# A hybrid state-space and attention block: two input buffers and an own output tile for the state-space units, units 14 steps apart, and the mixing's first loads two steps sooner

## The chip, the cores and the metric

The kernel runs on one core of a Trainium2 chip, whose engines work side by side: TensorE for matmuls (PE in the profile; its weight loads are PEld), VectorE (DVE), ScalarE (ACT), GpSimd (POOL), and SyncE (SP), which here issues most DMA transfers, one after the other. The metric is device time in microseconds, lower is better. The kernel before takes 2308.74 us, the median of three runs (2308.12 to 2310.45).

## What is computed

One layer on x of 2048 tokens by 1024, cut to what matters here:

```python
h = rmsnorm(x, norm_mix_g)
proj = h @ w_in                       # 512 columns u, then q, k, v of 512 each
# A: 32 groups of 16 channels, each with a complex diagonal state of 64
bu = einsum('bsgh,gph->bsgp', u, b_bar)
states = associative_scan(combine, (lam_bar, bu))
y = einsum('bsgp,ghp->bsgh', states, c_mat).real + d_skip * u
y = gelu(y)
y_ssm = y * sigmoid(y @ w_glu + b_glu)          # the GLU
# B: 8 heads; every chunk of 64 frames attends to itself and the 8 before it
y_att = chunked_attention(q, k, v, rel_bias)
x = x + concat(rmsnorm(y_ssm), rmsnorm(y_att)) @ w_out
h2 = rmsnorm(x, norm_ffn_g)
x = x + (silu(h2 @ w_gate) * (h2 @ w_up)) @ w_down
return rmsnorm(x, norm_final_g)
```

All is float32. A matmul is done as three matmuls on operands that are split into a rounded part and a rest (the names ending in h and l, or hi and lo).

## The kernel before

The projection of u comes first. Then `att_phase` runs the attention as 128 steps (token block, head pair, head, quarter of the block), with s as the number of the loop's turn. Each turn makes, in the order "sptf": the scores of step s (tile `sc`; bias and minimum on DVE, exp on ACT), every fourth turn the product of probabilities and V (`pj`) or its scaling, the transposes of step s − 2 (`pt`, one bank; ACT casts it to `pth`, DVE makes the rest `ptl`), and then "f": every `Unit` is advanced. A `Unit` is a generator with a number of yields n, a first turn s0 and an end s1: its yields are spread evenly over the turns from s0 to s1, and with `pre` its first piece comes that many turns ahead of s0. The units of the q, k and v projections (`pf`) are PE's filler between the attention steps. The order of PE is that of the code; the other engines' order is decided by the scheduler.

The state-space part is eight units of four groups each (`ssm_unit`). A unit loads its u into the tile `U`, and the weights `Bst`, `Tm` and `Vm`, all by SP (helper at L567, Tm and Vm at L576 to L581). After `YL` = 8 yields come the matmuls `pj<-U,Bst` (here "X"), copied by ACT into the tile `X` (L591). GpSimd scans it in seven local steps and fourteen more pieces (L605 to L617), DMAs put the shifted states into `XG` (L639), and after `YX` = 9 yields the matmuls `pj<-U,Tm` and `pj<-XG,Vm` ("Y") read U a second time. ACT copies them (L649) into a tile of the same tag as `X`, and SP stores it to y in DRAM in eight pieces (L652). The pool `sp` has one buffer for each tag, so U, and the tile that is X and then Y, are shared by all units. Unit b runs from turn 2 + 15b to turn 17 + 15b. X and Y use the two `pj` banks of the attention.

At turn `OPEN` = 119 the pool `aw` is given back and `mix_phase` begins; its first piece loads the gains and the GLU weights (`load_wg`, `sg` to `wgh` and `wgl`) and stops at a yield. At turn `GSTART` = 122 the pool `sp` is given back; from there the unit of the mixing runs, to turn 130. It loads the y of the first block in four pieces (`yr`, L1030), applies gelu (L1034, the second time for the block behind it), loads the attention's output `ya` (L1044, stored at L899) and the first `w_out` rows, yields `PY` = 8 times, and then gives PE one group of three GLU matmuls (`pf<-gh,wgh`) at a yield: 16 groups. The bias (L1061), one sigmoid over all groups and the product (L1065) end it. The row scaling of the attention's output is at L1082. Behind the attention the mixing goes on with the next block's GLU (`big`) and the norm's reciprocal root (L115 to L123).

Of the kernel before, what the change touches and what calls it, by code (L numbers as in the profile page):

```python
# [16 lines left out]
P = 128  # L17
# [3 lines left out]
NG, CH, NS = 32, 16, 64  # L21
NPR = NG // 2
L = 8
NC = SEQ // L
GB, GP = 4, 2
# [6 lines left out]
EPS = 1e-6  # L32
LAG = 2
WB = 3
OPEN, GSTART = 119, 122
R1 = 13
SGB = 2
ON_POOL = 2, 5, 7
# [6 lines left out]
SL = 1  # L45
LPH = 2
V0 = 0, 4
DB, XB = 3, 2
SW = 15
CUT = -8, -2, 2, 7, 13, 19, 24  # L50
CUTL = -8, -2, 2, 7, 13, 19, 23
ORDER = "sptf"
# [1 line left out]
YL = 8  # L54
YX = 9
# [504 lines left out]
def ssm_unit(k, p, psum, S, b, eng):  # L560

    nc = k.nc
    F = GB * CH
    U = k.t(p, "U", [P, GB, NC])

    def load(out, in_):
        ins = nc.sync.dma_start(out, in_)  # L567
        if b == 0:
            k.tc.keep_in_program_order(ins)

    for j in range(L):
        load(U[j * CH : (j + 1) * CH], S["u"][b * F : (b + 1) * F, j, :].rearrange("(g c) t -> c g t", c=CH))
    gs = slice(GB * b, GB * b + GB)
    bst = k.t(p, "Bst", [P, GB, P])
    load(bst[:].rearrange("p g m -> p (g m)"), S["bst"][b // 2][:, (b % 2) * GB * P : (b % 2 + 1) * GB * P])
    tm = k.t(p, "Tm", [P, GB, P])  # L576
    for i in range(L):
        load(tm[i * CH : (i + 1) * CH], S["kt"].rearrange("c g a m -> c g (a m)")[:, gs, P - CH * i : 2 * P - CH * i])
    vm = k.t(p, "Vm", [P, GB, P])
    load(vm[:], S["v"].rearrange("q g c n m -> (c n) (q g) m")[:, gs, CH:])  # L580
    for _ in range(YL):  # L581
        yield

    X = k.t(p, "X", [P, 2, GP, NC])
    for q in range(GP):
        ps = k.t(psum, "pj", [P, 2, NC], bufs=2)
        for g2 in range(2):
            k.ta.matmul(ps[:, g2, :], bst[:, 2 * q + g2, :], U[:, 2 * q + g2, :], start=True, stop=True)
        for g2 in range(2):
            for c in range(2):  # L590
                nc.scalar.copy(X[g2 * NS : (g2 + 1) * NS, c, q, :], ps[c * NS : (c + 1) * NS, g2, :])  # L591
        yield

    a8 = S["a8"]
    qs = slice(GP * b, GP * b + GP)
    Xk = X[:].rearrange("p r q (k s) -> p r q k s", s=8)
    Xe = Xk[:, :, :, :, 7].rearrange("p r q (a b) -> p r q a b", b=8)

    def step(dst, src, e, n):

        ar = a8[:, 0, qs, (0, 7, 15)[e]].unsqueeze(1).to_broadcast([P, 2, GP]).unsqueeze(3).to_broadcast([P, 2, GP, n])
        aw = S["sw"][:, e, :, qs].unsqueeze(3).to_broadcast([P, 2, GP, n])
        t = k.t(p, "st1", [P, 2, GP, NC // 8])
        t2 = k.t(p, "st2", [P, 2, GP, NC // 8])
        eng.tensor_tensor(t[:, :, :, :n], src, ar, op=ALU.mult)  # L605
        eng.tensor_tensor(t2[:, :, :, :n], src[:, ::-1], aw, op=ALU.mult)
        eng.tensor_tensor(dst, dst, t[:, :, :, :n], op=ALU.add)
        eng.tensor_tensor(dst, dst, t2[:, :, :, :n], op=ALU.add)

    def carry(dst, end, i0, n):  # L610

        for c in range(2):
            for e in range(2):
                t = k.t(p, "fx", [P, GP, NC // 8, 7])[:, :, :n]
                pw = a8[:, c if e == 0 else 1 - c, qs, i0 : i0 + 7].unsqueeze(2).to_broadcast([P, GP, n, 7])
                eng.tensor_tensor(t, end[:, e].unsqueeze(3).to_broadcast([P, GP, n, 7]), pw, op=ALU.mult)
                eng.tensor_tensor(dst[:, c], dst[:, c], t, op=ALU.subtract if e == 1 and c == 0 else ALU.add)  # L617
            yield

    for s in range(1, 8):  # L620
        step(Xk[:, :, :, :, s], Xk[:, :, :, :, s - 1], 0, NC // 8)
        yield
    for b_ in range(1, 8):
        step(Xe[:, :, :, :, b_], Xe[:, :, :, :, b_ - 1], 1, 4)
        yield
    for a in range(1, 4):
        step(Xe[:, :, :, a : a + 1, 7], Xe[:, :, :, a - 1 : a, 7], 2, 1)
        yield
    yield from carry(Xe[:, :, :, 1:, :7], Xe[:, :, :, :3, 7], 8, 3)
    yield from carry(Xk[:, :, :, 1:, :7], Xk[:, :, :, : NC // 8 - 1, 7], 0, NC // 8 - 1)  # L630

    if b == 0:
        k.XG = k.t(p, "XG", [P, GB, NC])
        nc.gpsimd.memset(k.XG[:, :, 0:1], 0.0)
    XG = k.XG
    XGv = XG[:].rearrange("p (q g) c -> p q g c", g=2)
    for g2 in range(2):
        for c in range(2):
            eng.dma_start(XGv[c * NS : (c + 1) * NS, :, g2, 1:], X[g2 * NS : (g2 + 1) * NS, c, :, : NC - 1])  # L639
    for _ in range(YX):  # L640
        yield
    Y = k.t(p, "X", [P, GB, NC])
    for q in range(GP):
        ps = k.t(psum, "pj", [P, 2, NC], bufs=2)
        for g2 in range(2):
            g = 2 * q + g2
            k.ta.matmul(ps[:, g2, :], tm[:, g, :], U[:, g, :], start=True, stop=False)
            k.ta.matmul(ps[:, g2, :], vm[:, g, :], XG[:, g, :], start=False, stop=True)
        nc.scalar.copy(Y[:, 2 * q : 2 * q + 2, :], ps[:])  # L649
        if q == GP - 1:  # L650
            for j in range(L):
                nc.sync.dma_start(S["y"][b * F : (b + 1) * F, j, :].rearrange("(g c) t -> c g t", c=CH), Y[j * CH : (j + 1) * CH])  # L652
        yield


SSM_N = YL + GP + 7 + 7 + 3 + 4  + YX + GP


class Unit:
# [21 lines left out]
def att_phase(k, ident, S):  # L681
    tc, nc, io = k.tc, k.nc, k.io
    with ExitStack() as cx:
# [245 lines left out]
        sp = tc.alloc_tile_pool(name="ssm", reuse_waits="tile", bufs=1)  # L929
        psum = cx.enter_context(tc.tile_pool(name="aps", bufs=1, space=bass.MemoryType.PSUM, reuse_waits="tile"))  # L930
        psum2 = cx.enter_context(tc.tile_pool(name="aps2", bufs=1, space=bass.MemoryType.PSUM, reuse_waits="tile"))
        units = []
# [9 lines left out]
                      Unit(qk_unit(sb, 2), QK_N, g0 + C[3], g0 + C[4], 2, light=LIGHT), Unit(v_unit(sb, 1), V_N, g0 + C[4], g0 + C[5], 2, light=LIGHT),  # L942
                      Unit(qk_unit(sb, 3), QK_N, g0 + C[5], g0 + C[6], 2, light=LIGHT)]
        for b in range(NG // GB):
            units.append(Unit(ssm_unit(k, sp, psum, S, b, k.ssm_eng), SSM_N, 2 + int(SW * b), 2 + int(SW * (b + 1)), light=SL))
        N = len(steps)
        for s in range(N + LAG + 2):
            if s == OPEN:
                aw.release()
                mix = mix_phase(k, S, lambda: k.t(pfs, "pf", [P, 512]))  # L950
                units += [Unit(islice(mix, MIX_N), MIX_N, GSTART, N + LAG, GSTART - OPEN)]
            if s == GSTART:
                sp.release()
            for o in ORDER:
                if o == "s" and s < N:
                    scores(steps[s])
                elif o == "t" and LAG <= s < N + LAG:
                    transp(steps[s - LAG])
                elif o == "p" and LAG + 1 <= s < N + LAG + 1 and steps[s - LAG - 1][3] == 3:
                    pv_head(steps[s - LAG - 1])  # L960
                elif o == "p" and s >= LAG + 2 and steps[s - LAG - 2][2:] == (1, 3):
                    pv_scale(steps[s - LAG - 2])
                elif o == "f":
                    for u in units:
                        u.advance(s)
        return mix


PY, PZ = 8, 1
MIX_N = 17 + PY + PZ  # L970


def mix_phase(k, S, bank):

    tc, nc, io = k.tc, k.nc, k.io
    te = k.te
    with ExitStack() as cx:
# [3 lines left out]
        gs, ga, bg = (k.t(mz, n, [P, 4]) for n in ("gs", "ga", "bg"))  # L981
# [40 lines left out]
        def load(sb, one=False):  # L1022
            b = B()
            b.o = {}
            yt = k.t(my, "ys", [P, 4, SB], bufs=2)
            b.ys, b.g = [yt[:, f] for f in range(4)], []
            if sb % 2 == 0:
                yrs[0] = k.t(my, "yr", [P, 4, L, 128])
                for f in range(4):
                    nc.sync.dma_start(yrs[0][:, f], S["y"][f * P : (f + 1) * P, :, sb * 64 : sb * 64 + 128])  # L1030
            yv = b.yr = yrs[0][:, :, :, (sb % 2) * 64 : (sb % 2 + 1) * 64]
            fs = [slice(0, 4)] if one else [slice(f, f + 1) for f in range(4)]
            for s in fs:
                nc.scalar.activation(yt[:, s].rearrange("p f (c j) -> p f c j", j=L), yv[:, s].rearrange("p f j c -> p f c j"), AF.Gelu_apprx_tanh)  # L1034
            for f in range(4):
                gh, gl = k.t(my, f"gh{f}", [P, SB], F32R), k.t(my, f"gl{f}", [P, SB], F32R)
                split(k, gh[:], gl[:], b.ys[f], nc.vector)
                b.g.append((gh, gl))
            return b
# [102 lines left out]
                    yield t[:, i * SB : (i + 1) * SB]  # L1142

        load_wg()
        yield
        mw = rx.enter_context(tc.tile_pool(name="mw", reuse_waits="tile", bufs=2, side="right"))
        wr = rx.enter_context(tc.tile_pool(name="wr", reuse_waits="tile", bufs=2, side="right"))
        b = load(0, True)
# [25 lines left out]
        psum, mx = k.psum, k.mx  # L1174
# [6 lines left out]
        for sb in range(NSB):  # L1181
# [39 lines left out]
            b = nxt  # L1221
# [483 lines left out]
```

## Time and profile before

| | us |
|---|---|
| median of three runs | 2308.74 |
| the profiled execution | 2304.9 |
| its span, first to last instruction | 2303.1 |
| scores of turn 119 begin | 684.84 |
| Y of unit 7 begins | 691.00 |
| first GLU matmul | 713.61 |
| first GLU matmul of the next block (`big`) | 743.35 |

Times inside the execution are from the start of the span. A timeline row gives start, duration, engine, line, operation, output and inputs with their shapes, and in brackets the idle time of the engine ahead of it and what ended that. "x8" merges eight instructions. In a row of windows each engine stands with its busy time, then the clock that TensorE was granted (1.00 is full), the DMA share and the transfer rate. Instructions that only wait or issue are not counted as busy.

### The profile page before, as it was taken

The numbers are of one execution on the slowest core, as the hardware profiler recorded it, in microseconds if no ns is written. First come the engines' busy times: TensorE is split into PE (matmuls) and PEld (weight loads), VectorE is DVE, ScalarE is ACT, GpSimd is POOL, SyncE is SP. The second block draws the span as 40 slices with busy tenths as digits, with TensorE's granted clock in tenths as the row PEclk, the third lists the DMA queues.
The fourth block names the chain that finished last, engine by engine and source line by source line (L and its number), as shares of the span: only waits on it lengthen the run. The fifth ranks groups of instructions, "written<-read, shape, count | busy, mean of one in ns | idle before, by whom it ended". The sixth has DMA issues, their size and how long they took to land.

```text
span 2303.1 us, 30454 instructions
## 1 busy us (share of the span) xinstructions
PE 2183.8 (95%) x10568; PEld 1834.1 (80%) x10568; DVE 1487.8 (65%) x2286; ACT 1001.3 (43%) x1675; POOL 1061.0 (46%) x1245
## 2 busy tenths in 40 slices
PE   8978799999997899989999999999999999999997
PEld 6667688898986788778888887888888878888886
DVE  7845555656555756676775669766645376578676
ACT  6335555555557542343333335333333343344332
POOL 3416655455660433265555554555555314445442
PEclk9989999999998999999999999999999999999998
DMA  8788766766653534754554556555433287465552
GB/s 295 260 286 265 235 210 204 207 190 193 192 137 114 178 118 163 249 165 143 167 193 157 205 190 254 195 193 167 158 96 110 76 326 265 165 228 183 201 182 74
DMA packets 216370, 437.00 MB, mean 190 GB/s; under 512 B 27352, under 2 KB 58120, under 8 KB 209112
## 3 DMA queue, kind: packets, MB, share of 16 engines
q1 hardware_dynamic: 211352, 420.89, 55.0%
q0 software_dynamic: 4864, 14.17, 1.9%
q8 instruction: 83, 1.36, 0.2%
q14 instruction: 71, 0.58, 0.1%
HBM read 294.98 MB, written 132.15 MB: 185 GB/s over the span
## 4 chain that ended last, share of the span: by engine, by line
PE 59%; DVE 3%; DMA 1%; ACT 1%; issue 1%; POOL 1%; SPq 0%; DVEq 0%; ACTq 0%; POOLq 0%
PE X L74 20%; PE ps L74 18%; PE Y L74 10%; PE big L74 6%; PE W L74 5%; DVE acc L1575 1%; DMA lo<-hc 0%; DMA x<-xt 0%; DVE xt L1117 0%; DVE lo L166 0%; DVE hd L166 0%; POOL c L166 0%; ACT hi L165 0%; POOL sa L1125 0%; DMA gl<-x 0%
## 5 line engine op out<-in xcount | busy, mean ns | idle before, releaser
L74 PE MATMUL X<-hi,c 128*128 128x512 f32 x1408 | 452.2, 392 | 7.6 <-ACT u L1391 3.5
L74 PE MATMUL ps<-hd,hd 128*128 128x512 f32 (+1 forms) x1968 | 431.7, 381 | 3.9 <-DVE hd L166 3.7
L74 PEld LDWEIGHTS ps<-hd,hd 128*128 128x128 f32 x1968 | 358.8, 190 | 75.5 <-DVE hd L166 5.1
L166 POOL TENSOR_TENSOR c<-S,c 128x512 fp32r<-128x512 f32 x176 | 253.1, 1440 | 260.7 <-ACT c L165 258.8
L74 PEld LDWEIGHTS X<-hi,c 128*128 128x128 f32 x1408 | 265.8, 189 | 65.2 <-ACT u L1391 5.1
L74 PE MATMUL X<-lo,c 128*128 128x512 f32 x704 | 275.3, 391 | 0.0
L166 POOL TENSOR_TENSOR hd<-hd 128x1536 fp32r<-128x1536 f32 (+1 forms) x46 | 159.1, 3463 | 232.0 <-ACT hd L165 218.8
L166 POOL TENSOR_TENSOR c<-raw,c 128x512 fp32r<-128x512 f32 x132 | 189.0, 1432 | 137.5 <-ACT c L165 109.1
L165 ACT CAST hd<-hd 128x1536 fp32r<-128x1536 f32 (+1 forms) x106 | 147.4, 1393 | 219.4 <-DMA hd<-hq 134.5
L74 PE MATMUL Y<-hi,c 128*128 128x512 f32 x704 | 225.5, 391 | 4.8 <-DVE u L1395 4.8
L1521 DVE TENSOR_TENSOR acc<-acc,ps 128x512 f32<-128x512 f32 x196 | 129.2, 681 | 79.5 <-PE ps L74 79.1
L74 PE MATMUL big<-m,woh 128*128 128x512 f32 x512 | 165.4, 404 | 0.6 <-DVE m L166 0.4
L165 ACT CAST c<-S 128x512 fp32r<-128x512 f32 x176 | 109.5, 622 | 116.5 <-PE Y L74 59.1
L74 PE MATMUL pf<-hi,w 128*128 128x512 f32 x416 | 150.9, 415 | 9.4 <-ACT hi L729 5.8
L74 PEld LDWEIGHTS Y<-hi,c 128*128 128x128 f32 x704 | 132.6, 188 | 33.9 <-DVE u L1395 6.3
L74 PEld LDWEIGHTS X<-lo,c 128*128 128x128 f32 x704 | 133.0, 189 | 27.7
L1391 ACT COPY u<-X 128x512 f32<-128x512 f32 x132 | 77.1, 585 | 177.5 <-PE X L74 177.5
L846 DVE CUSTOM_DVE_ANT_0 s<-sc,nb 128x640 f32<-128x640 f32 (+4 forms) x128 | 94.4, 737 | 89.4 <-PE sc L74 85.9
L605 POOL TENSOR_TENSOR st<-X,a 128x128 f32<-128x128 f32 (+2 forms) x136 | 47.4, 349 | 220.0 <-ACT X L591 157.4
L165 ACT CAST c<-raw 128x512 fp32r<-128x512 f32 x132 | 82.1, 622 | 143.1 <-PE Y L74 80.3
L166 DVE TENSOR_TENSOR hd<-hd 128x1536 fp32r<-128x1536 f32 (+1 forms) x60 | 119.3, 1990 | 31.2 <-ACT hd L165 30.5
L74 PE MATMUL Y<-lo,c 128*128 128x512 f32 x352 | 137.2, 390 | 0.0
(462 smaller groups left out, 4644.2 us busy)
## 6 DMA issues: line engine op xcount, KB each, us to landing
w<-wss SPq DMA_DIRECT2D x36, 1024.0 KB, 5.5
hq<-g SPq DMA_DIRECT2D x140, 256.0 KB, 2.1
hd<-hq SPq DMA_DIRECT2D x42, 768.0 KB, 4.5
hd<-wc SPq DMA_DIRECT2D x42, 768.0 KB, 6.0
raw<-in_w_gate SPq DMA_DIRECT2D x44, 512.0 KB, 3.7
raw<-in_w_up SPq DMA_DIRECT2D x44, 512.0 KB, 4.1
wc<-px SPq DMA_DIRECT2D x66, 256.0 KB, 3.2
wss<-w SPq DMA_DIRECT2D x12, 1024.0 KB, 5.6
```

The source lines that it names most:

```text
L74: return self.tc.keep_in_program_order(self.tc.nc.tensor.matmul(*a, **b))
L165: (hi_eng or nc.scalar).copy(hi, raw)
L166: (lo_eng or nc.gpsimd).tensor_tensor(lo, raw, f32(hi), op=ALU.subtract)
L605: eng.tensor_tensor(t[:, :, :, :n], src, ar, op=ALU.mult)
L846: nc.vector.tensor_tensor_reduce(s[:, :nk].rearrange("p (a b) -> p a b", a=nch), ps[:, :nch, :half], hd.nb[:, nk - 1 :: -1].rearrange("p ( ...
L1391: nc.scalar.copy(u[:], ps[:])
L1521: V.tensor_tensor(a, a, ps[:], op=ALU.add)
L1575: nc.vector.scalar_tensor_tensor(v, v, k.go[:, i : i + 1], self.rs[:, : self.n], op0=ALU.mult, op1=ALU.mult)
```

## The change

Two buffers of U, and a tag of its own for Y. In units 1 to 7 the loads of Tm and Vm are issued after the seven local scan steps, not at the unit's head, and the eight yields between head and X become one. Unit b now spans the turns 2 + 14b to 17 + 14b, with the head four turns ahead (unit 0 is as before). `sp` is given back at turn 119 with `aw`; the yield after `load_wg` is gone, so that the loads of y, of the attention's output and of w_out are issued at turn 119 too; the mixing's unit runs from turn 121 to 128, with `PY` = 3. A ring of descriptors for DMAs that GpSimd issues is 8192 bytes instead of the default.

```diff
@@ -32,7 +32,7 @@
 EPS = 1e-6
 LAG = 2
 WB = 3
-OPEN, GSTART = 119, 122
+OPEN, GSTART = 119, 121
 R1 = 13
 SGB = 2
 ON_POOL = 2, 5, 7
@@ -46,7 +46,7 @@
 LPH = 2
 V0 = 0, 4
 DB, XB = 3, 2
-SW = 15
+SW, SPAN = 14, 15
 CUT = -8, -2, 2, 7, 13, 19, 24
 CUTL = -8, -2, 2, 7, 13, 19, 23
 ORDER = "sptf"
@@ -561,7 +561,7 @@
 
     nc = k.nc
     F = GB * CH
-    U = k.t(p, "U", [P, GB, NC])
+    U = k.t(p, "U", [P, GB, NC], bufs=2)
 
     def load(out, in_):
         ins = nc.sync.dma_start(out, in_)
@@ -573,12 +573,17 @@
     gs = slice(GB * b, GB * b + GB)
     bst = k.t(p, "Bst", [P, GB, P])
     load(bst[:].rearrange("p g m -> p (g m)"), S["bst"][b // 2][:, (b % 2) * GB * P : (b % 2 + 1) * GB * P])
-    tm = k.t(p, "Tm", [P, GB, P])
-    for i in range(L):
-        load(tm[i * CH : (i + 1) * CH], S["kt"].rearrange("c g a m -> c g (a m)")[:, gs, P - CH * i : 2 * P - CH * i])
-    vm = k.t(p, "Vm", [P, GB, P])
-    load(vm[:], S["v"].rearrange("q g c n m -> (c n) (q g) m")[:, gs, CH:])
-    for _ in range(YL):
+    def load_tv():
+        tm = k.t(p, "Tm", [P, GB, P])
+        for i in range(L):
+            load(tm[i * CH : (i + 1) * CH], S["kt"].rearrange("c g a m -> c g (a m)")[:, gs, P - CH * i : 2 * P - CH * i])
+        vm = k.t(p, "Vm", [P, GB, P])
+        load(vm[:], S["v"].rearrange("q g c n m -> (c n) (q g) m")[:, gs, CH:])
+        return tm, vm
+
+    if b == 0:
+        tm, vm = load_tv()
+    for _ in range(YL if b == 0 else 1):
         yield
 
     X = k.t(p, "X", [P, 2, GP, NC])
@@ -620,6 +625,8 @@
     for s in range(1, 8):
         step(Xk[:, :, :, :, s], Xk[:, :, :, :, s - 1], 0, NC // 8)
         yield
+    if b:
+        tm, vm = load_tv()
     for b_ in range(1, 8):
         step(Xe[:, :, :, :, b_], Xe[:, :, :, :, b_ - 1], 1, 4)
         yield
@@ -639,7 +646,7 @@
             eng.dma_start(XGv[c * NS : (c + 1) * NS, :, g2, 1:], X[g2 * NS : (g2 + 1) * NS, c, :, : NC - 1])
     for _ in range(YX):
         yield
-    Y = k.t(p, "X", [P, GB, NC])
+    Y = k.t(p, "Y", [P, GB, NC])
     for q in range(GP):
         ps = k.t(psum, "pj", [P, 2, NC], bufs=2)
         for g2 in range(2):
@@ -653,7 +660,7 @@
         yield
 
 
-SSM_N = YL + GP + 7 + 7 + 3 + 4  + YX + GP
+SSM_N = 1 + GP + 7 + 7 + 3 + 4  + YX + GP
 
 
 class Unit:
@@ -942,15 +949,15 @@
                       Unit(qk_unit(sb, 2), QK_N, g0 + C[3], g0 + C[4], 2, light=LIGHT), Unit(v_unit(sb, 1), V_N, g0 + C[4], g0 + C[5], 2, light=LIGHT),
                       Unit(qk_unit(sb, 3), QK_N, g0 + C[5], g0 + C[6], 2, light=LIGHT)]
         for b in range(NG // GB):
-            units.append(Unit(ssm_unit(k, sp, psum, S, b, k.ssm_eng), SSM_N, 2 + int(SW * b), 2 + int(SW * (b + 1)), light=SL))
+            s0 = 2 + SW * b
+            units.append(Unit(ssm_unit(k, sp, psum, S, b, k.ssm_eng), SSM_N if b else SSM_N + YL - 1, s0, s0 + SPAN, 4 if b else 0, light=SL))
         N = len(steps)
         for s in range(N + LAG + 2):
             if s == OPEN:
                 aw.release()
+                sp.release()
                 mix = mix_phase(k, S, lambda: k.t(pfs, "pf", [P, 512]))
-                units += [Unit(islice(mix, MIX_N), MIX_N, GSTART, N + LAG, GSTART - OPEN)]
-            if s == GSTART:
-                sp.release()
+                units += [Unit(islice(mix, MIX_N), MIX_N, GSTART, N + 1, GSTART - OPEN)]
             for o in ORDER:
                 if o == "s" and s < N:
                     scores(steps[s])
@@ -966,8 +973,8 @@
         return mix
 
 
-PY, PZ = 8, 1
-MIX_N = 17 + PY + PZ
+PY, PZ = 3, 1
+MIX_N = 16 + PY + PZ
 
 
 def mix_phase(k, S, bank):
@@ -1142,7 +1149,6 @@
                     yield t[:, i * SB : (i + 1) * SB]
 
         load_wg()
-        yield
         mw = rx.enter_context(tc.tile_pool(name="mw", reuse_waits="tile", bufs=2, side="right"))
         wr = rx.enter_context(tc.tile_pool(name="wr", reuse_waits="tile", bufs=2, side="right"))
         b = load(0, True)
@@ -1692,7 +1698,7 @@
     import concourse.bacc as bacc
     from concourse.bass_utils import run_bass_kernel_spmd
 
-    nc = bacc.Bacc("TRN2", target_bir_lowering=False, num_devices=1)
+    nc = bacc.Bacc("TRN2", target_bir_lowering=False, num_devices=1, dynamic_dma_scratch_size=8192)
     arrays, io = {}, {}
     for name, a in layout(inputs).items():
         arrays[f"in_{name}"] = a
```

On PE, at the Y of unit 0 (turn 16). The last rows of its Y, and what follows (`pj<-U,Bst` is the X of unit 1). Before:

```order
761 L74 MATMUL pj_2553<-U_1864,Tm_1875 128x256
762 L74 MATMUL pj_2553<-XG_2387,Vm_1884 128x256
763 L74 MATMUL pj_2553<-U_1864,Tm_1875 128x256
764 L74 MATMUL pj_2553<-XG_2387,Vm_1884 128x256
765 L74 MATMUL sc_2567<-k_552_2112,q2h_2110 128x256
766 L74 MATMUL sc_2567<-k_552_2112,q2l_2111 128x256
```

and of the change:

```order
763 L74 MATMUL pj_2564<-U_1864,Tm_1875 128x256
764 L74 MATMUL pj_2564<-XG_2387,Vm_1884 128x256
765 L74 MATMUL pj_2579<-U_2393,Bst_2402 128x256 x2
766 L74 MATMUL pj_2586<-U_2393,Bst_2402 128x256 x2
767 L74 MATMUL sc_2599<-k_552_2112,q2h_2110 128x256
768 L74 MATMUL sc_2599<-k_552_2112,q2l_2111 128x256
```

The X of unit 1, which stood three turns behind this Y, now stands directly behind it, ahead of the next scores; so at every unit.

On SP, at the start of the mixing (turn 119 and behind; `in_w_glu` are GLU weights, `y` the state-space output in DRAM, `ya_s` the attention's). Before:

```order
357 L992 DMA sg_8226<-in_w_glu 128x512
358 L817 DMA nb_8299<-nbms_69 128x640
359 L1030 DMA yr_8351<-y_65 128x8x128 x2
360 L992 DMA sg_8232<-in_w_glu 128x512
361 L992 DMA sg_8238<-in_w_glu 128x512
362 L1030 DMA yr_8351<-y_65 128x8x128
363 L652 DMA y_65<-X_8277 16x4x256 x8
364 L899 DMA ya_s_66<-ya_8144 128x512
365 L1030 DMA yr_8351<-y_65 128x8x128
366 L1044 DMA ya_1937_8373<-ya_s_66 128x512
```

and of the change:

```order
371 L999 DMA sg_8248<-in_w_glu 128x512
372 L1037 DMA yr_8271<-y_65 128x8x128 x2
373 L999 DMA sg_8254<-in_w_glu 128x512
374 L999 DMA sg_8260<-in_w_glu 128x512
375 L1037 DMA yr_8271<-y_65 128x8x128 x2
376 L1051 DMA ya_1917_8293<-ya_s_66 128x512
```

The stores of unit 7's y and a store of the attention's output stood between the third and the fourth load of yr; they are now ahead of the whole group.

On ACT, around the first gelu (`ys<-yr`), where `s` is an exp, `pth` a probability cast and `gh` the cast of the GLU's input. Before:

```order
570 L864 CAST pth_8334<-pt_8336 128x5x128
571 L849 ACTIVATE s_8401,sm_8249<-s_8401,mn_8402 128x640
572 L864 CAST pth_8334<-pt_8412 128x5x128
573 L849 ACTIVATE s_8425,sm_8249<-s_8425,mn_8426 128x640
574 L864 CAST pth_8334<-pt_8429 128x5x128
575 L1034 ACT_TABLE_LOAD
576 L1034 ACTIVATE ys_8350<-yr_8351 128x2048
577 L1010 ACTIVATE sq_8381<-ya_1937_8373 128x512
578 L165 CAST gh_1929_8357<-ys_8350 128x512
```

and of the change:

```order
566 L871 CAST pth_8186<-pt_8343 128x5x128
567 L165 CAST wgh_1901_8252<-sg_8254 128x512
568 L165 CAST wgh_1904_8258<-sg_8260 128x512
569 L1041 ACT_TABLE_LOAD
570 L1041 ACTIVATE ys_8270<-yr_8271 128x2048
571 L1017 ACTIVATE sq_8301<-ya_1917_8293 128x512
572 L165 CAST gh_1909_8277<-ys_8270 128x512
...
578 L1041 ACTIVATE ys_8623<-yr_8271 128x2048
579 L1020 ACTIVATE sg_8309<-ya_1920_8296 128x512
580 L856 ACT_TABLE_LOAD
581 L856 ACTIVATE s_8362,sm_8323<-s_8362,mn_8363 128x640
```

The gelus stood behind the casts of turn 124; now they stand behind the cast of turn 121, and the exp of step 122 stands behind both. On PE the first GLU group stands, in the same way, ahead of the scores of step 122 instead of behind the transposes of turn 124. At the end of the attention the sigmoid and its table load stood behind the last `pth` cast on ACT and now stand ahead of it, and on DVE the row scaling at L1082 stands ahead of the `ptl` of the third-last step instead of the last.

## The prediction

> **What bounds the kernel now.** I read the busy shares first, then a table by windows, then TensorE's waits, and last the timelines of the places where those waits fall.
>
> ```profile
> PE 2183.8 (95%) x10568; PEld 1834.1 (80%) x10568; DVE 1487.8 (65%) x2286; ACT 1001.3 (43%) x1675; POOL 1061.0 (46%) x1245
> core 0: us, PE busy (x) PEld busy (x) DVE busy (x) ACT busy (x) POOL busy (x), PEclk, DMA share, GB/s
> 600.00:625.00 25.00, 25.00 (x146) 22.20 (x144) 14.95 (x27) 14.13 (x27) 17.26 (x43) 1.00 0.63 188
> 625.00:650.00 25.00, 22.28 (x128) 19.97 (x127) 10.07 (x17) 13.00 (x27) 2.64 (x6) 0.93 0.60 156
> 700.00:725.00 25.00, 13.30 (x48) 10.59 (x49) 11.24 (x27) 18.82 (x21) 1.28 (x1) 0.61 0.44 158
> 750.00:775.00 25.00, 19.73 (x86) 15.66 (x85) 24.46 (x35) 14.73 (x19) 16.97 (x8) 0.93 0.71 246
> ```
>
> PE (TensorE) bounds the kernel: 95% of the span, and all 25.00 us of a stretch such as 600 to 625. While attention has projections as filler, only a hole in PE's row can be won. 625 to 650 has one, of 2.72 us (25.00 less 22.28). Where attention runs out (700 to 725) PE does 13.30 us of work at a granted clock of 0.61, and from 750 on DVE (VectorE) is full, 24.46 of 25. The change touches both kinds of place, so they are priced apart.
>
> **Waits of the state-space units.** PE's waits up to 690 us (total, times, longest) and two places in its timeline:
>
> ```profile
> PE pj L74 <- DMA U<-u: 4.3, 2, 2.7
> PE pj L74 <- DMA Tm<-kts: 1.8, 2, 1.1
> PE pj L74 <- ACT X L591: 0.2, 1, 0.2
> 307.25 1.97 PE L74 MATMUL pj<-U,Bst 128*128 128x256 f32 x8 [1.60 <-DMA U<-u]
> 642.88 2.70 PE L74 MATMUL pj<-U,Bst 128*128 128x256 f32 x8 [2.72 <-DMA U<-u]
> ```
>
> A unit's U loads stand behind the Y matmuls of the unit before, the last readers of the one U buffer, and the X matmuls come too soon after them. With a second buffer, and loads that start four steps ahead, the rows on U, on Tm and on the copy of X go: 4.3 + 1.8 + 0.2 = **6.3 us**. After the wait of 2.72 the same eight matmuls take 2.70 us instead of 1.97, and that window's clock is 0.93; 0.07 of 25 us is **1.7 us** more. Together −8.0, as all of it lies in PE's filled stretch. What could be late next is Tm and Vm, now loaded after the seven local scan steps; Y needs them some seven steps later, and a step is about 3.2 us (below), so I count nothing.
>
> **What the change puts in PE's row there.** Unit 7's Y stood in the unfilled stretch and now comes seven steps sooner, among filler:
>
> ```profile
> 691.00 0.60 PE L74 MATMUL pj<-U,Tm 128*128 128x256 f32 x2
> ...
> 694.02 0.59 PE L74 MATMUL pj<-XG,Vm 128*128 128x256 f32 x2
> 695.04 0.39 PE L74 MATMUL pj<-pth,v 128*128 128x512 f32 x1
> ...
> 697.54 0.73 PE L77 MATMUL pt<-ident,s 128*128 128x128 f32 x5
> ```
>
> These eight pairs start every 0.43 us from 691.00 to 694.02: 8 × 0.43 = 3.45 us. Where they stood, PE waited soon after anyway; where they go it has no idle time. So **+3.45** before step 119, and what their going leaves behind is in the replay below.
>
> Also, a unit's Y and the next unit's X now stand back to back. They share the two pj banks, so the X matmuls wait for ScalarE's copies of Y:
>
> ```profile
> 629.03 0.59 ACT L649 COPY X<-pj 128x512 f32<-128x512 f32 x1 [2.42 <-PE pj L74]
> 630.71 0.59 ACT L649 COPY X<-pj 128x512 f32<-128x512 f32 x1 [1.10 <-PE pj L74]
> 644.09 3.03 ACT L591 COPY X<-pj 64x256 f32<-64x256 f32 x8 [3.93 <-issue]
> ```
>
> The second copy ends at 631.30, some 0.8 us after Y's last matmul of that unit, and one bank's X matmuls take 0.98 (half of 1.97), so PE arrives about then. The copies, 1.18 + 3.03 us of ACT in one step, also delay the next exp and probability cast. Bounds are 0 and 2 us over seven places; nearest is the 0.19 us that the one wait on such a copy cost, twice or three times: **+0.5**. The dense stretch then gains 8.0 − 3.45 − 0.5, about 4.0 us.
>
> **The hand-over to the mixing.** Before, on PE, ACT and SP's queue (the DMA issues):
>
> ```profile
> 684.84 0.31 PE L74 MATMUL sc<-k,q2h 128*128 128x320 f32 x1
> 701.72 1.00 PE L77 MATMUL pt<-ident,s 128*128 128x128 f32 x5 [2.42 <-DVE ptl L865]
> 705.54 1.30 PE L77 MATMUL pt<-ident,s 128*128 128x128 f32 x5 [1.75 <-DVE ptl L865]
> 713.61 0.79 PE L74 MATMUL pf<-gh,wgh 128*128 128x512 f32 x1 [6.76 <-ACT gh L165]
> 721.26 1.05 PE L74 MATMUL pf<-ones,sq 128*128 128x1 f32 x8 [1.47 <-DVE sq L1014]
> 730.94 0.31 PE L74 MATMUL sc<-k,q2h 128*128 128x320 f32 x1
> 734.15 0.71 PE L77 MATMUL pt<-ident,s 128*128 128x128 f32 x5
> 767.38 1.09 PE L77 MATMUL big<-ident,no 128*128 128x128 f32 x4 [5.11 <-DVE no L123]
> 707.59 1.28 ACT L1034 ACT_TABLE_LOAD   x1
> 708.88 3.64 ACT L1034 ACTIVATE ys<-yr 128x2048 f32<-128x2048 f32 x1
> 716.07 3.83 ACT L1034 ACTIVATE ys<-yr 128x2048 f32<-128x2048 f32 x1
> 692.70 0.53 SPq L1030 DMA_DIRECT2D yr<-y  x1
> 695.27 3.63 SPq L652 DMA_DIRECT2D y<-X  x8
> 702.77 0.53 SPq L1030 DMA_DIRECT2D yr<-y  x1
> yr<-y SPq DMA_DIRECT2D x8, 512.0 KB, 5.5
> ```
>
> The gelu needs all four yr loads. The fourth is issued at 702.77, behind unit 7's y stores and a ya_s store. Without these it follows the third, at about 693.3 to 694; with a median of 5.5 us to land that is 699.5. The order puts the gelu directly behind the cast of step 121, its table load hidden by the wait. Gelu from 700, and as now 4.73 us from its start to the first GLU matmul (713.61 − 708.88): near **704.7** against 713.61.
>
> But that is not 9 us won. PE now stands from 691.0, where the transposes of step 121 end and Y began, to 704.7, **13.7 us** at a stretch. Before, steps 122 to 124 were done inside that time, among them a set of probability-times-V matmuls (695.04 to 697.54, 2.5 us); they now come after the first GLU group. And the exp and the cast of step 122 stand behind the second gelu (3.83 us) and a table load (1.28) on ACT; the transposes of step 123 need the bank which that cast empties, and so come at about 717, some 3 us after PE is ready. From there to the transposes of step 128 are five steps of PE's work. A step with three GLU groups took 3.2 us (730.94 to 734.15), one with two 0.7 less; with 3, 2, 2, 3 and 2 groups that is 13.9, and 2.5 for probability times V, 1.05 for the token sums and about 1.2 for two sets of small transposes make 18.7. So **735.7**, 1.5 later than 734.15. That already counts the lost waits of 2.42, 1.75 and 1.47, Y's absence and the GLU groups done earlier.
>
> ```profile
> 741.65 1.92 ACT L1063 ACTIVATE yr<-yr 128x2048 f32<-128x2048 f32 x1
> 737.09 2.72 DVE L1082 SCALAR_TENSOR_TENSOR ya<-ya,ga,pf 128x512 f32<-128x512 f32 x4
> 741.12 2.48 DVE L166 TENSOR_TENSOR gl<-ys,gh 128x512 fp32r<-128x512 f32 x4
> ```
>
> In the tail the sigmoid and its table load, 1.28 + 1.92 = 3.2 us, stand ahead of the last probability cast instead of behind it, and PE's last attention matmuls and the first GLU of the next block wait for that. On the other side three of the four gl casts, 3 × 0.62 = 1.9, leave DVE's full stretch, whose end sets 767.38. So +3.2 − 1.9 = 1.3 more; behind 767.38 the order is as before. The hand-over costs +1.5 + 1.3 = **+2.8**. Its bounds are wide. Below: if none of the steps behind the pause costs more than now, the three waits lost, 2.42 + 1.75 + 1.47 = 5.6, come through whole, −5.6. Above: if the 3.2 and 2.72 us of row scaling (now ahead of the last casts on DVE) reach the join with the 1.5, +7.4.
>
> The clock in and behind this pause:
>
> ```profile
> 704.00:712.00 8.00, 1.30 (x5) 0.93 (x5) 2.22 (x4) 6.01 (x5) 0.00 (x0) 0.50 0.97 343
> ```
>
> The clock is 0.50 from 704 to 712, and over 700 to 725 it was 0.61. One pause of 13.7 us should cost about 5 us of half-speed work behind it, 2.5 us, about as much as now; the replay has it.
>
> The Trainium skill ("TensorE: Matmul & The Clock Gate", Part 1, the HAM clock gate) says the array falls to half rate after an idle window of about 3.4 us and returns after as much sustained work, which speaks against joining short pauses into a long one. The trace agrees with the half rate behind 6.76 us of waiting. By that page an estimate of the loss would be 1.7 us in place of 2.5, and the sum 0.8 lower.
>
> **Sum.** −6.3 − 1.7 + 3.45 + 0.5 + 2.8 = −1.25, on the profiled execution's 2304.9: 2303.65. That execution is 3.84 below the median of the three runs, 2308.74, so on the median's scale the forecast is **2307.5**. The halved ring for POOL's DMA descriptors gets nothing: POOL is busy 46%, and no row here waits for a ring.
>
> **Rivals.** *The pause shrinks as well.* If the steps behind the first GLU group cover its work so well that only the +3.45 is paid back, the 2.42, 1.75 and 1.47 us waits are gone and the join comes some 5.6 us sooner instead of 2.8 later: 2307.5 − 8.4 = 2299.1. For it: PE does only 13.30 us in 700 to 725. Against: exp of step 122 is held behind 3.83 + 1.28 us on ACT, and DVE is full around the join.
>
> *The order of the tail decides, slower.* One mechanism: the sigmoid ahead of the last cast, and DVE's row scaling ahead of the casts before it, hold PE's last transposes; DVE then starts its full stretch late. If none is absorbed, +3.2 + 2.7 + 1.5 = 7.4 at the join instead of 2.8, and 2 us at the seven doubled places instead of 0.5: 2307.5 + 4.6 + 1.5 = 2313.6. It decides once the first GLU matmul comes later than about 707, since DVE then has no slack left before the join.
>
> *The change does not free the loads.* SP issues in order:
>
> ```profile
> SPq L567 <- PE pj L74: 20.3, 5, 7.7
> ```
>
> SP stood 20.3 us for the old buffer. If another wait ahead of U in SP's queue takes its place, the 6.3 + 1.7 stay, and the time is 2307.5 + 8.0 = 2315.5. Against: four steps of lead are 4 × 3.2 = 12.8 us.
>
> **How the numbers follow.** Forecast 2307.5, chance 0.47; its own range is 2303 to 2312. Shrinking pause 0.30, slow tail 0.19, loads not freed 0.04. About 0.2%, 4.6 us, is what a measurement of this kernel can tell from no change, so faster is below 2304.1 and slower above 2313.4. The forecast gives 0.06 of its chance to faster and 0.03 to slower; the first rival 0.28 to faster and 0.02 to no change; the tail 0.13 to slower and 0.06 to no change; the last all to slower. That makes 0.34 faster, 0.46 same, 0.20 slower. The range that leaves two in ten out runs from the first rival, a little below it, to the two slower ones: 2298 to 2315.
>
> **What would show it.** Right: the rows of waits on U and Tm are gone from PE's waits, and windows from 300 to 675 are all full; unit 7's Y stands among filler; the first GLU matmul is near 700 (704.7 less the 4 won before), behind one idle row of 13 us or more (the same pause, shifted); and the row on the join's newton comes between 762 and 768. Wrong: waits on a copy of Y or X over 0.5 us at each of seven places; a GLU start that follows the yr landing by more than 6 us; or a join that comes before 760, which would mean that the hand-over gained where I have it losing.

## The result, and the profile after

The change is **slower**: 2351.84 us, the median of five runs (2348.33 to 2352.87), against 2310.45 for the kernel before beside it. The ratio is 1.0179, its 95% interval 1.0166 to 1.0192. The profiled execution's span is 2349.9 us against 2303.1, 46.8 more. First the busy shares of the page of after, then two windows of its table by 100 us and the one stretch from turn 16 to turn 120, and last the same stretch before (PE busy, PEld, DVE, ACT, POOL, then the granted clock).

```profile
PE 2195.9 (93%) x10568; PEld 1841.4 (78%) x10568; DVE 1492.7 (64%) x2286; ACT 1001.3 (43%) x1675; POOL 1059.9 (45%) x1245
200.00:300.00 100.00, 73.79 (x373) 59.58 (x371) 50.91 (x116) 44.78 (x116) 56.03 (x124) 0.86 0.61 191
600.00:700.00 100.00, 98.11 (x633) 90.27 (x632) 55.48 (x100) 54.65 (x108) 54.02 (x140) 0.98 0.60 182
217.70:729.70 512.00, 460.01 (x2723) 408.57 (x2721) 272.62 (x503) 259.29 (x541) 252.90 (x619) 0.95 0.62 188
```

```profile
216.00:687.20 471.20, 441.31 (x2707) 396.02 (x2705) 271.07 (x503) 257.74 (x538) 255.84 (x619) 0.99 0.66 197
```

The loss lies where I had a gain, in the attention. The same stretch takes 512.0 us instead of 471.2. PE's idle time in it is 52.0 instead of 29.9, and its busy time grew by 18.7; 3.45 of that is the Y of unit 7, which came in, and the other 15 are the same matmuls at a lower clock (0.95 against 0.99). The start of the scores of each turn, read from PE's timeline, shows where:

| turn | before, us | after, us | later by |
|---|---|---|---|
| 16 | 216.0 | 217.7 | 1.8 |
| 20 | 237.1 | 247.6 | 10.5 |
| 32 | 292.2 | 319.0 | 26.8 |
| 48 | 361.9 | 390.5 | 28.6 |
| 60 | 419.9 | 453.3 | 33.5 |
| 88 | 540.8 | 581.0 | 40.2 |
| 120 | 687.2 | 729.7 | 42.5 |
| join (`big<-ident,no`) | 767.38 | 812.62 | 45.2 |
| span | 2303.1 | 2349.9 | 46.8 |

What PE waits for in that stretch of after (total, times, longest):

```profile
PE pf L74 <- ACT hi L736: 10.6, 5, 4.3
PE pf L74 <- DMA w<-wss: 10.4, 5, 3.5
PE sc L74 <- DVE k L782: 8.5, 3, 4.0
PE pf L74 <- DVE lo L727: 5.7, 5, 2.3
PE sc L74 <- DVE mn L853: 4.9, 4, 1.8
PE pj L74 <- DMA XG<-X: 3.8, 1, 3.8
...
PE pf L74 <- ACT w L165: 2.4, 1, 2.4
PE pj L74 <- ACT Y L656: 0.8, 1, 0.8
...
```

and before, of the same names (from 216 to 687.2; there is no row on w):

```profile
PE sc L74 <- DVE k L775: 6.8, 3, 2.9
PE pf L74 <- ACT hi L729: 5.8, 2, 3.5
...
PE pj L74 <- DMA XG<-X: 1.4, 1, 1.4
PE sc L74 <- DVE mn L846: 0.3, 1, 0.3
PE pf L74 <- DVE lo L720: 0.2, 1, 0.2
```

The rows on U and Tm are gone, as forecast. But the filler itself (`pf`) now waits: for hi and lo, the parts of x's rows, and for w, the projections' weights, 26.7 us where there had been 6.0. The waits on XG and on the minimum `mn` grew by 2.4 and 4.6 us. The casts to hi and lo wait themselves for x's rows (xt), which are loaded late. SP's queue shows why, first before and then after (start, duration of issuing, line, transfer):

```profile
210.64 1.87 SPq L693 DMA_DIRECT2D raw<-in_w_qk  x2
215.62 0.93 SPq L714 DMA_DIRECT2D xt<-in_xt  x2
...
225.15 3.61 SPq L652 DMA_DIRECT2D y<-X  x8
```

```profile
216.05 0.93 SPq L709 DMA_DIRECT2D wss<-w  x2
230.93 3.60 SPq L659 DMA_DIRECT2D y<-Y  x8
234.57 0.90 SPq L700 DMA_DIRECT2D raw<-in_w_qk  x2
...
249.06 0.50 SPq L721 DMA_DIRECT2D xt<-in_xt  x1
```

Before, the raw qk weights and the first rows of x were issued ahead of the stores of unit 0's Y. Now the store stands ahead of them. SP issues in order, and from 217.0 to 230.9 it stood there, 13.9 us, until ACT had copied Y; the qk weights went out at 234.57 instead of 210.64. U's eight loads, whose buffer is free early, are issued from 198.66 on instead of 224.10, and the projections' loads moved behind the store. PE's part of it, 8 us further on:

```profile
242.62 0.50 PE L74 MATMUL pf<-hi,w 128*128 128x512 f32 x1 [2.45 <-ACT w L165]
243.88 1.22 PE L74 MATMUL pf<-hi,w 128*128 128x512 f32 x2 [0.53 <-DVE w L166]
271.07 0.80 PE L74 MATMUL pf<-hi,w 128*128 128x512 f32 x1 [4.33 <-ACT hi L736]
```

Behind such a wait a 512-column matmul takes 0.6 to 0.8 us instead of 0.39. In two windows of 3.41 us around the first of them PE is busy for 0.92 us of the one, and the granted clock is 0.50 in the next:

```profile
239.99:243.40 3.41, 0.92 (x4) 0.30 (x2) 2.43 (x6) 3.10 (x6) 3.10 (x7) 1.00 0.32 112
243.40:246.81 3.41, 2.93 (x7) 2.35 (x8) 1.84 (x2) 0.12 (x1) 3.25 (x5) 0.50 0.67 269
```

SP's own waits on Y, from 100 to 760 us of after, and then the row on the copy before (100 to 730 us):

```profile
SPq L659 <- ACT Y L656: 28.8, 8, 13.9
SPq L567 <- PE pj L74: 18.1, 3, 10.4
```

```profile
SPq L652 <- ACT X L649: 7.6, 5, 3.1
```

Before, the unit loads waited 20.3 us. So the unit loads gave up hardly any wait: Tm, whose tile still has one buffer, waits for Y in U's place.

### The profile page after: what moved, and what is told of

It reads as the page before. It is cut to its first block, busy times and chain, and to the rows that moved or that the text cites. A ratio compares the mean times of both kernels' runs of the same rounds, so it can differ in the third digit from the quotient of the medians.

```text
span 2349.9 us, 30421 instructions
## 1 busy us (share of the span) xinstructions
PE 2195.9 (93%) x10568; PEld 1841.4 (78%) x10568; DVE 1492.7 (64%) x2286; ACT 1001.3 (43%) x1675; POOL 1059.9 (45%) x1245
## 4 chain that ended last, share of the span: by engine, by line
PE 56%; DVE 4%; DMA 2%; POOL 1%; issue 1%; ACT 0%; SPq 0%; DVEq 0%; ACTq 0%; POOLq 0%
PE X L74 19%; PE ps L74 18%; PE Y L74 9%; PE big L74 6%; PE W L74 5%; DVE lo L166 1%; DVE acc L1581 1%; POOL c L166 0%; DMA x<-xt 0%; DVE xt L1124 0%; DVE g L1444 0%; DMA raw<-in_w_up 0%; DVE hd L166 0%; DVE u L1401 0%; DMA hc<-gh 0%
## 6 DMA issues: line engine op xcount, KB each, us to landing
raw<-in_w_gate SPq DMA_DIRECT2D x44, 512.0 KB, 3.7
raw<-in_w_up SPq DMA_DIRECT2D x44, 512.0 KB, 4.0
```

## The experiments

Three theories stood against each other. **A**: waits in SP's queue. Stores of Y and loads of Tm stand, waiting for Y, ahead of the projections' loads. **B**: the smaller descriptor ring slows the loads. **C**: X directly behind Y, and units 14 turns apart, cost PE the time by themselves. "Turn 120" below is how much later than in the kernel before its scores begin in the profiled execution (before: 687.2).

**1. The ring alone, on the kernel before.**

```diff
-    nc = bacc.Bacc("TRN2", target_bir_lowering=False, num_devices=1)
+    nc = bacc.Bacc("TRN2", target_bir_lowering=False, num_devices=1, dynamic_dma_scratch_size=8192)
```

> The kernel before with only the descriptor ring of GpSimd's DMAs cut to 8192 bytes. Theory A (SP issues in order; stores of Y and loads of Tm now stand ahead of the projections' loads and hold them while they wait for Y): no change, 2309 us within 3. Theory B (the smaller ring slows the loads): +30 to +45, near 2350. Theory C (Y and the next X back to back, 14 turns apart, cost PE the time by themselves): no change.

2307.9 us, ratio 0.9989 (0.9977 to 1.0001). B falls. In the one execution that was profiled turn 120 nevertheless comes 5.2 us later than in the kernel before, so a difference of some 5 us at turn 120 between two traces shows nothing by itself.

**2. The units' part of the change without the mixing's.**

```diff
-OPEN, GSTART = 119, 121
+OPEN, GSTART = 119, 122
-                sp.release()
...
+            if s == GSTART:
+                sp.release()
-PY, PZ = 3, 1
-MIX_N = 16 + PY + PZ
+PY, PZ = 8, 1
+MIX_N = 17 + PY + PZ
         load_wg()
+        yield
```

(The mixing's unit ends at N + LAG again.)

> The change without its mixing part (mixing from turn 122 with eight empty yields as before, pool of the units given back at 122). All theories put the loss into the attention, where turn 120 comes 42.5 us late: 2344 to 2350. If the mixing part carried the loss it would be near 2309.

2348.47 us, ratio 1.0159 (1.0134 to 1.0183), turn 120 at +42.1. The units carry the loss, as far as the intervals tell: that of the change (1.0166 to 1.0192) overlaps this one.

**3 and 4. The change, with the stores of Y on GpSimd's queue; then Tm and Vm of units 1 to 7 too.**

```diff
-                nc.sync.dma_start(S["y"][b * F : (b + 1) * F, j, :]...
+                eng.dma_start(S["y"][b * F : (b + 1) * F, j, :]...
```

```diff
-            load(tm[i * CH : (i + 1) * CH], S["kt"]...
+            (eng.dma_start if b else load)(tm[i * CH : (i + 1) * CH], S["kt"]...
-        load(vm[:], S["v"]...
+        (eng.dma_start if b else load)(vm[:], S["v"]...
```

> The change with the eight stores of each Y issued by GpSimd instead of SP. Theory A: SP's waits of 28.8 us on the copy of Y go, and what stood behind them comes earlier; the waits of Tm on Y remain (18.1 us): 2318 to 2338. Theory B: GpSimd issues more through the small ring, 2350 or more. Theory C: no change, 2347 to 2355.

> As the run before, with the loads of Tm and Vm of units 1 to 7 issued by GpSimd too, behind its seven local scan steps. Theory A: SP no longer waits for Y at all, 2302 to 2320, and PE's waits on hi, lo and w are back to those of the kernel before (about 6 us). Theory B: 2350 or more. Theory C: 2347 to 2355.

2332.72 us (ratio 1.0093, 1.0073 to 1.0114) and 2325.65 (1.0062, 1.0040 to 1.0085); turn 120 at +22.2 and +14.0. Nothing of the computation or of PE's order differs from the change, so what these two moves gain lies in how the DMAs are issued. The first came as A had it; the second is 6 us above A's range. What is left of PE's waits in the second (195 to 730 us):

```profile
PE pj L74 <- DMA XG<-X: 5.5, 1, 5.5
PE pf L74 <- DMA w<-wss: 4.2, 2, 3.3
PE pf L74 <- DVE lo L727: 2.0, 1, 2.0
PE pf L74 <- ACT hi L736: 1.5, 1, 1.5
```

The waits on hi and lo are down from 16.3 to 3.5. Some 12 of the +14 arises between turns 16 and 20. There PE waits 5.5 us for unit 0's XG instead of 1.45 and 3.7 us for a `ptl`, and the granted clock is 0.85 where it was 1.00. U's loads still stand ahead of two 1 MB weight stores in SP's order; that these, issued late, run beside XG and slow it is argued, not shown (run 5 still waits up to 4.4 us for an XG).

**5. All unit DMAs of units 1 to 7 on GpSimd.**

```diff
-        ins = nc.sync.dma_start(out, in_)
+        ins = (eng if b else nc.sync).dma_start(out, in_)
```

(With the stores of Y as in run 3.)

> The change with all unit DMAs of units 1 to 7 (U, Bst, Tm, Vm and the stores of Y) issued by GpSimd. SP's order of the projections' loads is then that without units. Theory A: the 14 us that were left at turn 120 with U and Bst on SP go too, turn 120 within 4 us of the kernel before, total 2300 to 2314 with the hand-over's 4. Theory C: turn 120 stays 14 us late or more, 2322 or more; the same if GpSimd's queue becomes the limit.

2311.49 us, ratio 1.0002 (0.9990 to 1.0015), turn 120 at +3.5. With SP free of units 1 to 7, 39 of the 42.5 us at turn 120 are gone, and PE's order is still that of the change. What PE waits for now (215.3 to 690.7 us) shows the rows on w and mn gone and hi and lo small, while XG has grown:

```profile
PE pj L74 <- DMA XG<-X: 8.1, 2, 4.4
...
PE pf L74 <- DVE lo L727: 1.7, 2, 1.5
...
PE pf L74 <- ACT hi L736: 1.0, 1, 1.0
...
```

The +3.5 is a net figure: the waits on U and Tm went (−8.0 by the prediction) and the Y of unit 7 came (+3.45). So C can hold some 8 us in this form, but not 42.

**6. Only the buffers, on the kernel before.**

```diff
-    U = k.t(p, "U", [P, GB, NC])
+    U = k.t(p, "U", [P, GB, NC], bufs=2)
-    Y = k.t(p, "X", [P, GB, NC])
+    Y = k.t(p, "Y", [P, GB, NC])
```

(With the ring of run 1.)

> The kernel before with two buffers of U, an own tile for Y and the 8192-byte ring, and nothing else of the change: units 15 turns apart, Tm and Vm at the head. PE's waits on U (6.3 us with their clock 8.0) should go. Theory A (SP's order): the second buffer alone lets the scheduler put U's loads and the store of Y ahead of the loads of xt on SP, so hi and lo come late and part of the loss appears already: 2312 to 2330. Theory C (spacing and Y next to X): none of these is here, so 2298 to 2305.

2319.63 us, ratio 1.0042 (1.0028 to 1.0056). The buffers take PE's waits on U away and still make the kernel slower by themselves. PE waits 16.4 us for hi and lo, 6.0 before, and SP's wait on the copy of Y is there already (195 to 725 us):

```profile
SPq L652 <- ACT Y L649: 24.4, 7, 13.0
SPq L567 <- PE pj L74: 10.7, 2, 6.9
```

**7. The units' part, 15 turns apart.**

```diff
-SW, SPAN = 14, 15
+SW, SPAN = 15, 15
```

(On run 2.)

> The change without its mixing part and with units 15 turns apart, so that no X stands directly behind a Y. Theory A: SP's order is nearly that of the change (store of Y ahead of the qk weights and xt), so most of the loss stays: 2330 to 2350. Theory C: 2300 to 2312.

2322.3 us, ratio 1.0051 (1.0033 to 1.0068), turn 120 at +16.6. A miss for both theories, between their ranges: 26 us less than 14 apart, though SP's waits on the copy of Y are longer here (36.0 us). PE's waits on `w<-wss` are down to 0.3, and SP's for Y ahead of Tm are 6.9 instead of 18.1. Either theory could claim that; run 13 puts it to the test.

**8. Control: the stores of Y on GpSimd in the kernel before** (the edit of run 3).

> Control: the kernel before with only the stores of Y issued by GpSimd. Theory A: SP's waits on Y in the kernel before are 7.6 + 3.5 us and mostly harmless, so 2303 to 2310; a gain of 15 us or more would mean that the move itself, not the order of the change, made the gain of the run with the stores on GpSimd.

2304.85 us, ratio 0.9978 (0.9967 to 0.9990). The move by itself gains some 5 us, not 19, so some 14 of run 3's gain belong to the order of the change.

**9 and 10. The buffers with the stores on GpSimd (runs 6 and 3 together); the units' part with all unit DMAs on GpSimd (runs 2 and 5 together).**

> Two buffers of U and an own tile for Y in the kernel before, with the stores of Y on GpSimd. Theory A (waits in SP's queue): of the 10 us that the buffers cost, the 24.4 us of SP's waits on the copy of Y go; Tm and Vm still stand there, waiting for Y: 2302 to 2314. If the buffers cost the time in another way: 2318 or more.

> The change without its mixing part and with all unit DMAs of units 1 to 7 on GpSimd. It differs from the earlier run with all of them on GpSimd only by the mixing. If the hand-over of the change costs 4 us, as the traces have it (span 46.8 later, turn 120 42.5 later), 2305 to 2310 against 2311.5; if the mixing part gains, 2314 or more.

2314.31 us, ratio 1.0015 (1.0002 to 1.0028), just above A's range. Against run 6 the move gains 5 us, as it does without the buffers (run 8). Against run 8, which has the stores on GpSimd too, the buffers still cost 9.5 us (2304.85 to 2314.31), as they do on SP. So the place of the stores is not what the buffers' loss comes from. PE's waits on hi and lo are down to 7.4 us; SP's for Y ahead of Tm rose from run 6's 10.7 to 19.5, and PE's on `mn` are 6.8 against 2.3 in run 8. What of this costs the time stays open. The second gave 2309.03, ratio 0.9987 (0.9972 to 1.0001), as expected, but its trace does not show the mixing as the reason: from turn 120 (+3.7) to the end of its span (+7.6) it loses 3.9 us, as run 5 does (+3.5 to +7.2). What the mixing part costs stays unclear by these two.

**11. The change, with each store of Y on SP, but three turns later in the program.**

```diff
-            for j in range(L):
-                nc.sync.dma_start(S["y"]...
+            def store():
+                for j in range(L):
+                    nc.sync.dma_start(S["y"]...
+            k.stores.append(store)
...
+                    late += [(s + 3, st) for st in k.stores]
+                    k.stores = []
                     for u in units:
                         u.advance(s)
+                    for st in [st for due, st in late if due == s]:
+                        st()
```

> The change with each store of Y still on SP but issued three turns later in the program, so that in SP's order the qk weights stand ahead of it; the Tm and Vm loads now come ahead of it too. Theory A: a good part of the 19 us that moving the stores to GpSimd gave: 2325 to 2342. If it is the queue that carries the store and not its place: 2347 or more.

2340.18 us, ratio 1.0126 (1.0104 to 1.0148): 11.7 us less than the change on the same queue, so the place in the order counts. The rest stays; SP now waits for Y at Tm instead, which may be why:

```profile
SPq L567 <- PE pj L74: 23.2, 5, 10.5
SPq L660 <- ACT Y L656: 8.8, 1, 8.8
```

**12. The buffers with all unit DMAs on GpSimd, 15 turns apart** (runs 6 and 5 together).

> The kernel before with two buffers of U, an own tile for Y, the 8192-byte ring and all unit DMAs of units 1 to 7 (U, Bst, Tm, Vm, stores of Y) on GpSimd; units 15 turns apart and the mixing as before. Theory A: SP carries no unit DMA, so the 10 us that the buffers cost go and PE's waits on U (8.0) as well; a later XG for unit 0 gives some 5 back: 2300 to 2308, against 2304.85 of the kernel before with only the stores moved. If GpSimd's queue is now the bound: 2312 or more, with PE's waits on XG or U over 8 us.

2314.13 us, ratio 1.0007 (0.9993 to 1.0020). No gain. PE's row on U is gone, but this stands in its place:

```profile
PE pj L74 <- DMA XG<-X: 14.0, 5, 5.2
```

The other case of the expectation came: 2312 or more, with over 8 us on XG. Why XG is late is not shown. GpSimd, which issues XG too, waits 62.1 us for Y ahead of Tm over seven units here, but in run 13 it waits 82.2 us there, and PE's wait on XG is 4.4 us. What differs is that Tm and Vm are loaded at a unit's head here, and behind the local scan steps there, with the head four turns ahead.

**13 and 14. The units' part 15 turns apart with all unit DMAs on GpSimd (runs 7 and 5); the kernel before with stores, Tm and Vm on GpSimd.**

> The change without its mixing part, units 15 turns apart, all unit DMAs of units 1 to 7 on GpSimd. If the spacing acts only through SP's queue, this equals the run 14 apart with the same queue (2309.0): 2304 to 2314, turn 120 within 4 us of its 691.0. If X directly behind Y and the spacing cost PE time by themselves, the 26 us between the two spacings on SP come back here: 2285 to 2300.

> The kernel before with the stores of Y and the loads of Tm and Vm of units 1 to 7 on GpSimd; U and Bst stay on SP. Theory A: as the run with the stores alone (2304.85) or 1 to 3 us better, since nothing of a unit but U waits for Y in SP's queue: 2300 to 2306. If GpSimd's queue delays XG or the scan, 2308 or more.

The first gives 2302.6 us, ratio **0.9960** (0.9943 to 0.9978), and the lowest of all, though its interval overlaps that of run 8 (0.9967 to 0.9990). It lies between the two expected ranges; turn 120 comes 3.2 us sooner than before and 7.0 sooner than in run 10. That does not measure the 4.0 us which the prediction worked out for the dense stretch: here Y of unit 7 begins at 687.8, behind turn 120, and no X stands directly behind a Y, so that its −8.0 alone would apply. Of the 26 us between the two spacings on SP some 6 remain (0.9960 against 0.9987, intervals that touch): most of the spacing's cost went through SP's queue, and a small part may be its own. The second gives 2307.75, ratio 0.9985 (0.9973 to 0.9997), 1.75 us above A's range: no better than the stores alone. The kernel before with all unit DMAs of units 1 to 7 on GpSimd was not run, so of the 40 us that run 5 gains, some 4 to 5 may come with the move itself, as in runs 8 and 14, and not from the change's order.

## Why the prediction was wrong

The forecast was 2307.5 and the range ended at 2315; it is 2351.84.

- **The waits on U and Tm (−8.0).** They went, as said. The step that failed is the sentence behind it: "What could be late next is Tm and Vm", with nothing counted. I looked for what was late on PE in the unit, and not for what stands behind the units' DMAs in SP's queue. Shown in its place: hi, lo and w of the projections, 26.7 us of PE's waits where there had been 6.0, and 15 us of lower clock on top. Runs 3, 4 and 5 take 20, 28 and 39 us of it back at turn 120 by moving the units' DMAs to GpSimd's queue alone, of which the move by itself is worth some 5 (run 8). Which edit puts the store where it does harm is in part open: the buffers alone cost some 10 us (run 6), and as much with the stores on GpSimd (run 9); the units' part costs 12 us at 15 turns (run 7) and 39 at 14 (run 2).
- **The rival that came nearest** ("The change does not free the loads") had the right queue and the wrong victim. It let SP's wait hit the U loads, priced at 8.0 us and 0.04, and did not ask who else stands in that queue. I read the order of SP at turn 119, for yr; at turn 16 it has the store ahead of `raw<-in_w_qk` and xt.
- **Y of unit 7 (+3.45).** Right: from 705.30 on it runs among filler, eight pairs 0.43 us apart.
- **Y and X back to back (+0.5).** Right in size as far as the copies go: one wait of 0.8 us on a copy of Y. Between runs 10 and 13 spacing and this order make 6.4 us together; with unit 7's Y ahead of turn 120 only in the first (3.45), some 3 us are left, which these runs cannot tell from nothing.
- **The hand-over (+2.8).** The number came out: the join is 45.2 us late where turn 120 was 42.5 late, +2.7; to the end of the span it is +4.3. Two of its parts were off against each other, so that is in part luck, and runs 5 and 10 lose the same 4 us from turn 120 on with the mixing's part and without it. Its parts, in the trace of after:

```profile
742.92 1.28 ACT L1041 ACT_TABLE_LOAD   x1 [3.27 <-DMA yr<-y]
744.21 3.64 ACT L1041 ACTIVATE ys<-yr 128x2048 f32<-128x2048 f32 x1
748.93 0.80 PE L74 MATMUL pf<-gh,wgh 128*128 128x512 f32 x1 [15.32 <-ACT gh L165]
748.90:755.40 6.50, 6.46 (x19) 5.47 (x20) 3.91 (x7) 6.50 (x7) 1.28 (x1) 0.50 0.06 22
812.62 0.62 PE L77 MATMUL big<-ident,no 128*128 128x128 f32 x4 [1.32 <-DVE no L123]
```

The first GLU matmul comes 19.2 us behind the scores of turn 120; I had 17.5. The pause is 15.32 us, not 13.7, most of it because the table load (1.28 us) is not hidden by the wait on yr: it starts only when yr has landed. The stretch from there to the join is shorter than forecast by about as much. Behind the pause PE works 6.5 us at a clock of 0.50, which costs some 3.2 us where the prediction had 2.5.

On clock and queue the measurements differ from two pages of the Trainium skill. The waits here were at most 4.3 us each, and one of 2.45 us was enough (the row at 242.62 and the clock of 0.50 from 243.40 on); 22.1 us more idle time came with some 15 us of slower matmuls. The Trainium skill ("TensorE: Matmul & The Clock Gate", Part 1, the HAM clock gate) has the rate fall after an idle window of about 3.4 us; by that most of these waits would have cost only themselves. The Trainium skill also says ("DMA: Bandwidth & Descriptors", Issuing engines are not separate DMA queues) that issuing from several engines saves only the issuing time, usually small beside the transfer. By the runs it saved 40 us here (2351.84 to 2311.49), since what stood in the queue was not issuing but waits (28.8 and 18.1 us on SP).

## What to carry to other kernels

When a change frees a buffer, read the order of the queue that issues the loads, not only the engine that waited: a DMA that waits there holds all behind it, and with a scheduler the freed load changes who that is. Price the wait by what the bounding engine needs from the rows behind it. A store that waits for a result of the bounding engine is better issued from a queue that carries nothing that engine will need soon, and the loads that wait for the same result with it, if that queue has time: here that paid in the change (runs 3 to 5), and for the loads in the kernel before it did not (run 14). And a move needs its control: run 9 beside run 6 looks like a cure for the buffers' loss, and beside run 8 it is none.

## What was not expected of the hardware

- Short waits cost PE some 1.7 times their length here: 22.1 us more idle time and about 15 us of lower clock in the same stretch.
- A descriptor ring of 8192 bytes for GpSimd's DMAs instead of the default changed nothing that can be measured (0.9989, 0.9977 to 1.0001).
- The table load ahead of the gelu started at 742.92, when the gelu's input had landed, and the gelu at 744.21: it was not done during the 3.27 us of waiting.
